# Squared-ReLU MLP of a two-block network: products of all 512 tokens, a freer boundary, and smaller settings

## The chip, the cores and the metric

The kernel runs on one core of a Trainium2 chip. Its five engines are TensorE (PE in the profile; its loads of the stationary operand are the row PEld), VectorE (DVE), ScalarE (ACT), GpSimd (POOL) and SyncE (SP), which issues most of the weight transfers. The metric is the device time of one execution in microseconds (us); lower is better. Everything is in 32-bit floats. TensorE multiplies in a shorter format, so each operand is kept as two parts, a rounded one (`hi`) and the rest (`lo`), and each product is three matmuls: hi x hi, hi x lo and lo x hi.

## The reference

Two transformer blocks run one after the other on 512 tokens of width 1024. The first has two attention forms side by side, attention to a memory and a SwiGLU MLP; the second has an mLSTM mixer, a squared-ReLU MLP, latent attention (MLA) and a second squared-ReLU MLP. The second block's norms are shifted and scaled by rows that are worked out from a condition vector. What matters here:

```
def sqrelu_mlp(h, w1, w2):
    return jnp.square(jax.nn.relu(h @ w1)) @ w2          # 1024 -> 4096 -> 1024
...
        ada = cond @ ada_w[l] + ada_b[l]
        sh1, sc1, g1, sh2, sc2, g2 = jnp.split(ada, 6, axis=-1)
...
        x = x + g1[:, None, :] * rmsnorm(y, norm_g[l, 1])
        h = modulate(rmsnorm(x, norm_g[l, 2]), sh2, sc2)
        y = sqrelu_mlp(h, mlp_w1[l], mlp_w2[l])
        x = x + g2[:, None, :] * rmsnorm(y, norm_g[l, 3])
```

The MLP appears twice (l = 0 and l = 1), with its own weights each time. The change touches the up projection `h @ w1` of l = 0.

## The kernel before, in words

Tokens come in four tiles of 128 (t = 0 to 3), features in tiles of 128 (k). The residual stays in SBUF as `x[t]`. The normalised, transposed input of a stage, `h` or `hn`, is either an `HT` (all 512 tokens in each buffer) or an `HS` (tokens 0 to 255 and 256 to 511 in buffers of their own). Such buffers, and the split weight tiles, come from one pool of 14 large buffers (`s8`); `HT` takes four of them when tile 0 is put, `HS` two then and two with tile 2.

**Weights.** `pump` loads raw weight tiles in the order of use and plans their splitting into hi (ScalarE) and lo (VectorE): `split` for plain tiles (L307 and L308, or L317 and L318 with a gain), `split7` for the seven-product form (L341, L342, and sums of weight quarters in L345 and L361). `wcap` bounds the split tiles that are alive; `lc` sets it for the last down projection of an MLP. While `quiet` is set, one piece is emitted about every two products.

**Products.** `prod` (L447 to L449) issues three matmuls for each k. An up projection of a squared-ReLU MLP takes pairs of hidden tiles. The first pairs go through `relu_pairs`, in halves of 256 tokens at the boundary. The later ones, when `h` is an `HS`, go through `wino`: the product of a 2 x 2 grid of blocks in seven products instead of eight, each of 4 k x 3 matmuls of 256 columns (L510), whose results VectorE and ScalarE combine (L520 to L534); `quarters` prepares the sums of token quarters, partly on GpSimd (L482). The choice stands in two lines:

```
        toks = (slice(0, 256), slice(256, S)) if halves or isinstance(h, HS) else (ALL,)
...
                by7 = k0 and isinstance(h, HS)
```

The 32 hidden tiles come in blocks of 6, 8, 6, 6 and 6; behind each block's up projection stands its part of the down projection, with sums in `acc` (L1358). The first block is always computed by `relu_pairs`.

**Boundaries.** `boundary` runs the last products of a stage tile by tile: `a` updates the residual (L648) and computes the next norm (squares L579, then GpSimd L568 and L562), `scaled` scales the row (L598), `put` transposes it on TensorE (L608), applies gain and shift if there are any (L616 on VectorE, L619 on ScalarE) and splits it (L626, L627). Products of the next stage (`first`) come between. Before, all of it stands inside `ordered()`: the order of PE, ACT, DVE and POOL is the written one. Outside such a region the framework's scheduler orders each engine's instructions by priority and a simulated time; `hot("hb")` raises the priority by 300 instructions.

**Row steps.** `ada` works out the condition rows in the background: `row_by` multiplies and adds weight rows on VectorE (L863), sums over partitions by one matmul (L881) and writes the row to DRAM; `cols_steps` reads some rows back as columns (transpose L386, copy L388). `step` makes one background step each time the products since the last have cost more than `pace` (`pacb` from the mLSTM on), except while `quiet` is set. `crow` and `gcol` force the steps that are still missing.

`all` calls the stages in order; the part that the change touches begins at `self.late = True`.

Of the kernel before, what the change touches and what calls it, by code (L numbers as in the profile page):

```python
# [20 lines left out]
P = 128  # L21
S = 512
NT = 4
DM = 1024
KD = 8
# [5 lines left out]
D_FF = 2816  # L31
ALL = slice(0, S)

BUF = dict(s8=14, u2=15, row=2, raw=4, w0=4, w1=4, w2=4, w3=5, w4=5, w5=5, w6=5, w7=5, ps=8, pace=2.0, pacb=2.0, man=0, lag=3, lagx=3, lagm=3, half=1, quiet=1, xp=0, fp=2, r1=1.25, r1b=3.6, r1c=2.4, r2=1.6, r2b=2.6, rx=1.4, rm=0.6, pre=10, gl=3, pl=0, hb=300, hs=0, ha=0, sp=0, spq=1.3, sq=1, b1=1, b2=1, lc=7, ar=4, mb=(6, 8, 6, 6, 6), mc=(4, 3, 4, 4, 4), st2=1, pr2=8, z1=4.5, z2=5, gt=3, rv=2, gs=1, rl=3, n1=4, ex=2, em=3, vg=1, sb=(8, 8, 6), mo=4, x1=2, g0=20, st=1, y1=0, y2=1, y3=0, ph=0, pq=0, fy=1, u1=6, s32=4, sm=60)

TWO_PI = 2.0 * np.pi

# [1 line left out]
def tt(t):  # L39
    return slice(t * P, (t + 1) * P)  # L40
# [98 lines left out]
class Net:  # L139
# [52 lines left out]
    def hot(self, key):  # L192
        n = BUF[key]
        return nullcontext() if self.dry or not n else self.tc.high_priority(offset=n)
# [181 lines left out]
    def cols_steps(self, name, srcs, eng=None):  # L376
        n = sum(k for _, k in srcs)
        r = self.u2((n, P))
        o = 0
        for src, k in srcs:  # L380
            (eng or self.nc.gpsimd).dma_start(out=r[o:o + k, :], in_=src.rearrange("(k p) -> k p", p=P))
            o += k
        for _ in range(3):
            yield None
        ps = self.bank((P, n))
        self.nc.tensor.transpose(out=ps, in_=r, identity=self.ident[:n, :n])  # L386
        c = self.t(f"cols_{name}", [P, n], F32, 1)
        self.nc.vector.tensor_copy(out=c, in_=ps)  # L388
        yield c
# [211 lines left out]

    def put(self, ys, h, k, t, mod=None):

        for y, cw in ys:
            n = cw // P
            ps = self.bank((P, n, P))
            for j in range(n):
                self.nc.tensor.transpose(out=ps[:, j, :], in_=y[:, tt(j)], identity=self.ident)  # L608
            hi, lo = h.blk(k, n, tt(t))
            if mod:  # L610
                g, sh = mod
                y = self.u2((P, n, P))
                for j in range(n):
                    gj, sj = (c[:, k + j:k + j + 1] for c in (g, sh))
                    if j < 2:
                        self.nc.vector.tensor_scalar(out=y[:, j, :], in0=ps[:, j, :], scalar1=gj, scalar2=sj,  # L616
                                                     op0=ALU.mult, op1=ALU.add)
                    else:
                        self.nc.scalar.activation(y[:, j, :], ps[:, j, :], AF.Identity, scale=gj, bias=sj)  # L619
                ps = y  # L620
            self.parts(hi, lo, ps)
            k += n

    def parts(self, hi, lo, x, scale=None):
        if scale is None:
# [5 lines left out]
                                                op0=ALU.mult, op1=ALU.subtract)  # L631


    def boundary(self, y_of, nxt, first, late=(1, 1, 2)):

# [3 lines left out]
        pend, rs = {}, {}  # L641
# [11 lines left out]
        def scaled(t):  # L653
            pend[t] = nxt(t, rs[t])

        with self.ordered():
            for t in range(NT):
                g, n = y_of(t), 0
                while True:
                    try:  # L660
                        next(g)
                    except StopIteration as e:
                        ys, ss = e.value
                        break
                    n += 1
                    if n == 4 and nxt and t >= 2:
                        self.put(*pend.pop(t - 2))
                if nxt and t >= 1:
                    scaled(t - 1)
                rs[t] = a(t, ys, ss)  # L670
            if nxt:
                i = -1
                for i, need in enumerate(first):
                    if i == late[0]:
                        scaled(NT - 1)
                    for n, t in ((1, NT - 2), (2, NT - 1)):
                        if i == late[n]:
                            self.put(*pend.pop(t))
                assert not pend, (i, late)
        self.quiet = False  # L680

# [379 lines left out]
    def mixer1(self):  # L1061
        nc, V, a = self.nc, self.nc.vector, self.a
        w = a["w_in"][0]
        self.x = [self.const(f"x{t}", [P, DM]) for t in range(NT)]
        get = lambda t: nc.sync.dma_start(out=self.x[t], in_=a["x"][0, tt(t), :])
# [8 lines left out]
            nc.sync.dma_start(out=ext[:, 64:256], in_=rb)  # L1074
            nc.sync.dma_start(out=far, in_=rb[:, 191:192].rearrange("h o -> (h o)").partition_broadcast(P))

        self.before = {2: [lambda: get(1)], 4: [lambda: get(2), lambda: get(3)], 6: [biases]}
        h = HT(self, KD)
        vf = self.big([P, NT, S])
        with self.in_order():  # L1080
# [7 lines left out]
        c = self.u2((8, S))  # L1088
# [104 lines left out]
        for t in range(NT):  # L1193
            ys = []
# [136 lines left out]
        return ho  # L1331


    def mlp(self, blocks, up, w_down, g, nxt, first, ready=None, caps=None):

        nc, V = self.nc, self.nc.vector
        acc = [[self.u2() for _ in range(2)] for _ in range(NT)]
# [1 line left out]
        for b, nb in enumerate(blocks):  # L1339
# [26 lines left out]
            if last:  # L1366
# [6 lines left out]
                        ms += part(t, c, (yield from product(t, wgs[c])))  # L1373
                    return acc[t], ms

                self.boundary(y_of, nxt, first)
            else:
                for c in range(2):
                    wg = self.weights(w_down, k0, nb, c * S, S)
# [59 lines left out]
    def relu2(self, h, l, g, nxt, first, ready=None):  # L1439
# [23 lines left out]
                quarters.extend(self.quarters(h))  # L1463

        quarters = []
        self.mlp(BUF['mb'], up, self.a["mlp_w2_2"][l], g, nxt, first, ready, BUF['mc'])


    VW = 129
# [408 lines left out]
    def all(self):  # L1878
# [13 lines left out]
        h = hn  # L1892
# [13 lines left out]
        self.late = True  # L1906
        self.cap(5)
        g = self.crow(2)
        hn = HS(self, KD)
        self.out_lin(a["a_w_out_2"][0], ho, g, nxt(4, 3, hn), self.relu_pairs(hn, a["mlp_w1_2"][0], 0, BUF["fp"], True), "head")  # L1910
        self.dumps(4)
        h = hn
# [64 lines left out]
```

## Time and profile before

| | |
|---|---|
| median of 3 runs | 2026.44 us (2026.16 to 2029.08) |
| the profiled execution's own time | 2028.55 us |
| its span, first to last instruction | 2026.5 us |
| mean granted clock of TensorE | 0.985 |
| busy: TensorE, VectorE, ScalarE, GpSimd | 1943.2, 1373.4, 1073.1, 355.6 us |
| moved by DMA | 242.01 MB, 119 GB/s |

The profiled execution lies 2.1 us above the median of the runs, and its time 2.05 us above its span. Matmuls overlap in the profile, so a busy TensorE is not one at its peak: what it could save shows as idle time before an instruction, and as a granted clock under 1. Stretches of the span in this kernel: SwiGLU MLP about 480 to 836, mLSTM 836 to 1030, its output and boundary 1030 to 1112, first squared-ReLU MLP 1112 to 1441, its boundary to 1482, MLA to 1633, its output and boundary to 1688, second squared-ReLU MLP to the end.

### The profile page before, as it was taken

The page shows a single profiled execution, that of the slowest core. Times are in us where ns is not written, and L with a number is a line of the kernel's source. Part 1 is how long each engine was busy: PE and PEld are TensorE (multiplying, and loading weights), DVE is VectorE, ACT ScalarE, POOL GpSimd, SP SyncE. Part 2 cuts the span into 40 slices and gives each one's busy share as a digit, 9 for nine tenths or more (in the row PEclk, how much of TensorE's full clock was granted, in tenths as well). Part 3 has the DMA queues.
Part 4 walks back from the last instruction along what each step waited for, and adds up shares of the span by engine and source line. Part 5 has one row for each costly group of instructions (what it writes and reads, how often), then busy time and mean ns, then how long its engine had stood idle before and what let it go on. Part 6 is the DMA issues. An engine that isn't in the chain of part 4 may idle for free. (4 is left out here: it accounts for less than half of the span.)

```text
span 2026.5 us, 29742 instructions
## 1 busy us (share of the span) xinstructions
PE 1943.2 (96%) x10738; PEld 1663.4 (82%) x10738; DVE 1373.4 (68%) x2689; ACT 1073.1 (53%) x2355; POOL 355.6 (18%) x711
## 2 busy tenths in 40 slices
PE   7999999999999999899999899998889989999997
PEld 5888988878888888678888788888687879989996
DVE  5756655856666665576866888898568747657665
ACT  6767775545353243556446464455465556545543
POOL 1331111201122211121323221222120012000000
PEclk9999999999999999999999999999999999999999
DMA  6322342523465554153442354565243212233321
GB/s 198 89 79 65 113 136 74 187 73 115 136 208 177 161 172 116 52 169 101 154 135 84 110 162 138 185 188 165 62 114 94 84 63 73 73 114 105 104 85 62
DMA packets 175251, 242.01 MB, mean 119 GB/s; under 512 B 20108, under 2 KB 117537, under 8 KB 175105
## 3 DMA queue, kind: packets, MB, share of 16 engines
q1 hardware_dynamic: 150704, 170.53, 27.2%
q0 software_dynamic: 24400, 69.60, 11.5%
q8 instruction: 84, 1.38, 0.3%
q14 instruction: 63, 0.51, 0.1%
HBM read 237.88 MB, written 2.20 MB: 118 GB/s over the span
## 5 line engine op out<-in xcount | busy, mean ns | idle before, releaser
L447 PE MATMUL ps<-s,s 128*128 128x512 f32 (+4 forms) x2276 | 863.0, 381 | 26.7 <-ACT s L626 25.1
L448 PE MATMUL ps<-s,s 128*128 128x512 f32 (+4 forms) x2276 | 851.6, 375 | 2.8 <-DVE s L627 1.9
L449 PE MATMUL ps<-s,s 128*128 128x512 f32 (+4 forms) x2276 | 849.7, 375 | 1.5 <-DVE s L627 1.4
L447 PEld LDWEIGHTS ps<-s,s 128*128 128x128 f32 (+2 forms) x2276 | 432.0, 190 | 105.9 <-ACT s L626 31.0
L449 PEld LDWEIGHTS ps<-s,s 128*128 128x128 f32 (+2 forms) x2276 | 431.2, 190 | 83.2 <-DVE s L627 5.2
L448 PEld LDWEIGHTS ps<-s,s 128*128 128x128 f32 (+2 forms) x2276 | 432.3, 190 | 79.1 <-DVE s L627 4.0
L510 PEld LDWEIGHTS ps<-s,s 128*128 128x128 f32 x2184 | 261.8, 188 | 6.7 <-DVE u L526 4.5
L510 PE MATMUL ps<-s,s 128*128 128x256 f32 x2184 | 263.7, 281 | 3.6 <-DVE u L526 3.6
L307 ACT ACTIVATE s<-raw 128x512 fp32r<-128x512 f32 x277 | 157.8, 622 | 143.2 <-PE ps L449 97.9
L308 DVE TENSOR_TENSOR s<-raw,s 128x512 fp32r<-128x512 f32 x277 | 190.3, 726 | 57.0 <-ACT s L307 55.7
L863 DVE SCALAR_TENSOR_TENSOR u<-araw,cond,u 128x512 f32<-128x512 f32 x224 | 167.3, 747 | 24.2 <-DMA araw<-in_ada_w 15.4
L317 ACT ACTIVATE s<-raw,cols_all 128x256 fp32r<-128x256 f32 (+1 forms) x305 | 143.5, 546 | 66.5 <-PE ps L449 29.8
L318 DVE SCALAR_TENSOR_TENSOR s<-raw,cols_all,s 128x256 fp32r<-128x256 f32 (+1 forms) x305 | 147.6, 538 | 39.3 <-ACT s L317 38.7
L868 POOL DMA_DIRECT2D araw<-in_ada_w x192 | 104.0, 542 | 338.0 <-DVE u L863 289.2
L627 DVE TENSOR_TENSOR s<-u,s 128x512 fp32r<-128x512 f32 x126 | 87.0, 700 | 79.4 <-ACT s L626 56.7
L626 ACT ACTIVATE s<-u 128x512 fp32r<-128x512 f32 x126 | 77.6, 625 | 63.8 <-PE ps L449 31.9
L568 POOL TENSOR_SCALAR sm<-sm,sm 128x1 f32<-128x1 f32 x34 | 10.5, 307 | 527.5 <-ACT junk L579 527.4
L341 ACT ACTIVATE s<-raw 128x512 fp32r<-128x512 f32 x104 | 62.7, 621 | 72.7 <-PE ps L449 37.6
L627 DVE TENSOR_TENSOR s<-ps,s 128x512 fp32r<-128x512 f32 (+3 forms) x100 | 59.1, 606 | 42.4 <-ACT s L626 35.0
L341 ACT ACTIVATE s<-u 128x512 fp32r<-128x512 f32 x78 | 48.7, 624 | 66.8 <-DVE u L345 36.4
L342 DVE TENSOR_TENSOR s<-raw,s 128x512 fp32r<-128x512 f32 x104 | 70.7, 683 | 15.4 <-ACT s L341 15.1
L1358 DVE TENSOR_TENSOR u<-ps,u 128x512 f32<-128x512 f32 x80 | 53.9, 685 | 34.3 <-PE ps L449 33.6
(261 smaller groups left out, 2162.9 us busy)
## 6 DMA issues: line engine op xcount, KB each, us to landing
raw<-in_mlp_w SPq DMA_DIRECT2D x128, 512.0 KB, 3.8
araw<-in_ada_w POOLq DMA_DIRECT2D x192, 256.0 KB, 3.5
raw<-in_w_gate_up SPq DMA_DIRECT2D x44, 512.0 KB, 4.1
raw<-in_w_in SPq DMA_DIRECT2D x24, 512.0 KB, 4.2
raw<-in_a_w_in SPq DMA_DIRECT2D x24, 512.0 KB, 3.8
raw<-in_w_down SPq DMA_DIRECT2D x22, 512.0 KB, 3.7
raw<-in_w_mem_kv SPq DMA_DIRECT2D x16, 512.0 KB, 3.6
araw<-in_kv_ada_w POOLq DMA_DIRECT2D x32, 256.0 KB, 4.0
```

The costliest lines, as they stand in the source:

```text
L307: A.activation(hi[:, sl, cl], src[:, sl, cl], AF.Copy)
L308: f.tensor_tensor(out=lo[:, sl, cl], in0=src[:, sl, cl], in1=hi[:, sl, cl].bitcast(F32), op=ALU.subtract)
L317: A.activation(hi[:, i, :], src[:, i, :], AF.Copy, scale=g)
L318: V.scalar_tensor_tensor(out=lo[:, i, :], in0=src[:, i, :], scalar=g, in1=hi[:, i, :].bitcast(F32), op0=ALU.mult, op1=ALU.subtract)
L341: A.activation(hi, x, AF.Copy)
L447: self.nc.tensor.matmul(ps, lhsT=ah, rhs=bh, start=first and i == 0, stop=False)
L448: self.nc.tensor.matmul(ps, lhsT=ah, rhs=bl, start=False, stop=False)
L449: self.nc.tensor.matmul(ps, lhsT=al, rhs=bh, start=False, stop=last and i == n - 1)
L510: nc.tensor.matmul(ps, lhsT=l[:, k, :], rhs=m[:, k, :], start=first and k == e == 0, stop=k == 3 and e == 2, skip_group_check=True)
L627: self.nc.vector.tensor_tensor(out=lo, in0=x, in1=hi.bitcast(F32), op=ALU.subtract)
L863: V.scalar_tensor_tensor(out=acc, in0=raws.pop(j), scalar=vec[:, j:j + 1], in1=acc, op0=ALU.mult, op1=ALU.add)
L868: nc.gpsimd.dma_start(out=raws[j], in_=ws[:, j, :])
```

## The change

In `BUF`, `pace` and `pacb` go from 2.0 to 1.9 and `lc` from 7 to 6. `cols_steps` lets five steps pass instead of three between reading a row and transposing it. `put` scales both halves of a tile, in the buffers they came in, before it splits the first. `boundary` gets a form without a written order (`fixed=False`), which the first squared-ReLU MLP's boundary uses; there the scaling of the last tile comes before the next stage's first product, and a tile is put when a product needs it. The x tiles are loaded one weight load earlier at the start. `hn` of the first squared-ReLU MLP becomes an `HT`, so its `relu_pairs` after the boundary take all 512 tokens in one product, and `wino` and `quarters` are no longer used there. The second MLP keeps them.

```diff
...
-        for _ in range(3):
+        for _ in range(5):
             yield None
...
     def put(self, ys, h, k, t, mod=None):
 
+        todo = []
         for y, cw in ys:
             n = cw // P
             ps = self.bank((P, n, P))
             for j in range(n):
                 self.nc.tensor.transpose(out=ps[:, j, :], in_=y[:, tt(j)], identity=self.ident)
-            hi, lo = h.blk(k, n, tt(t))
             if mod:
                 g, sh = mod
-                y = self.u2((P, n, P))
+                y = y.rearrange("p (n c) -> p n c", c=P)
...
                 ps = y
+            todo.append((k, n, ps))
+            k += n
+        for k, n, ps in todo:
+            hi, lo = h.blk(k, n, tt(t))
             self.parts(hi, lo, ps)
-            k += n
...
-    def boundary(self, y_of, nxt, first, late=(1, 1, 2)):
+    def boundary(self, y_of, nxt, first, late=(1, 1, 2), fixed=True):
...
-        with self.ordered():
+        hot = nullcontext if fixed else lambda: self.hot("hb")
+        with self.ordered() if fixed else nullcontext():
             for t in range(NT):
                 g, n = y_of(t), 0
...
-                    if n == 4 and nxt and t >= 2:
+                    if n == 4 and nxt and t >= 2 and fixed:
                         self.put(*pend.pop(t - 2))
-                if nxt and t >= 1:
-                    scaled(t - 1)
-                rs[t] = a(t, ys, ss)
+                with hot():
+                    if nxt and t >= 2 and not fixed:
+                        self.put(*pend.pop(t - 2))
+                    if nxt and t >= 1:
+                        scaled(t - 1)
+                    rs[t] = a(t, ys, ss)
             if nxt:
-                i = -1
+                if not fixed:
+                    with hot():
+                        scaled(NT - 1)
                 for i, need in enumerate(first):
-                    if i == late[0]:
+                    if fixed and i == late[0]:
                         scaled(NT - 1)
-                    for n, t in ((1, NT - 2), (2, NT - 1)):
-                        if i == late[n]:
-                            self.put(*pend.pop(t))
+                    for t in sorted(pend):
+                        if t <= need if not fixed else i >= late[t - 1]:
+                            with hot():
+                                self.put(*pend.pop(t))
...
-        self.before = {2: [lambda: get(1)], 4: [lambda: get(2), lambda: get(3)], 6: [biases]}
+        self.before = {1: [lambda: get(1)], 3: [lambda: get(2), lambda: get(3)], 6: [biases]}
...
-    def mlp(self, blocks, up, w_down, g, nxt, first, ready=None, caps=None):
+    def mlp(self, blocks, up, w_down, g, nxt, first, ready=None, caps=None, fixed=True):
...
-                self.boundary(y_of, nxt, first)
+                self.boundary(y_of, nxt, first, fixed=fixed)
...
-        self.mlp(BUF['mb'], up, self.a["mlp_w2_2"][l], g, nxt, first, ready, BUF['mc'])
+        self.mlp(BUF['mb'], up, self.a["mlp_w2_2"][l], g, nxt, first, ready, BUF['mc'], fixed=nxt is None)
...
         g = self.crow(2)
-        hn = HS(self, KD)
+        hn = HT(self, KD)
         self.out_lin(a["a_w_out_2"][0], ho, g, nxt(4, 3, hn), self.relu_pairs(hn, a["mlp_w1_2"][0], 0, BUF["fp"], True), "head")
```

## Rows read from the trace of the kernel before

**Rows 1.** The page: busy us of each engine, share of the span, instructions.

```profile
PE 1943.2 (96%) x10738; PEld 1663.4 (82%) x10738; DVE 1373.4 (68%) x2689; ACT 1073.1 (53%) x2355; POOL 355.6 (18%) x711
```

**Rows 2.** Windows: length, busy us (instructions) PE, PEld, DVE, ACT, POOL, clock, DMA.

```profile
630.00:680.00 50.00, 50.00 (x218) 40.52 (x217) 30.39 (x52) 15.89 (x32) 8.95 (x18) 1.00 0.47 149
1089.00:1115.00 26.00, 25.94 (x222) 25.73 (x220) 16.95 (x22) 17.55 (x34) 12.27 (x8) 1.00 0.29 90
1121.00:1441.00 320.00, 304.27 (x1813) 267.94 (x1814) 269.61 (x458) 153.63 (x288) 68.29 (x130) 0.97 0.51 157
1688.00:1987.00 299.00, 295.80 (x1886) 267.23 (x1886) 202.81 (x343) 157.60 (x293) 9.87 (x6) 1.00 0.30 92
```

**Rows 3.** Waits of TensorE from 1112 to 1441: us in total, times, longest.

```profile
PE ps L386 <- DMA u<-arow: 5.8, 2, 4.7
PE ps L447 <- ACT s L626: 5.5, 3, 3.3
PE ps L881 <- DVE u L627: 4.4, 2, 3.6
PE ps L510 <- DVE u L526: 3.6, 3, 1.7
PE ps L449 <- DVE s L627: 1.4, 1, 1.4
```

**Rows 4.** Waits of TensorE from 1441 to 1482.

```profile
PE ps L608 <- ACT u L598: 8.8, 2, 7.5
```

**Rows 5.** Windows around the longest waits, columns as in rows 2.

```profile
1117.00:1125.00 8.00, 4.06 (x11) 3.25 (x12) 7.83 (x13) 1.45 (x3) 1.51 (x3) 0.57 0.01 1
1407.00:1412.00 5.00, 4.78 (x15) 3.83 (x16) 4.15 (x9) 1.09 (x3) 1.01 (x3) 0.66 0.59 177
1417.00:1429.00 12.00, 7.20 (x19) 4.80 (x18) 8.85 (x15) 4.85 (x11) 2.14 (x4) 0.57 0.68 204
1469.00:1480.00 11.00, 5.67 (x25) 5.68 (x26) 5.96 (x21) 5.23 (x12) 1.33 (x4) 0.53 0.62 144
```

**Rows 6.** Chain of waits in the second MLP: start, us, what.

```profile
1887.64 25.44 PE ps L510 x216
```

**Rows 7.** Groups of VectorE from 1121 to 1441: busy us, mean ns, idle before.

```profile
L342 DVE TENSOR_TENSOR s<-raw,s 128x512 fp32r<-128x512 f32 x52 | 35.4, 681 | 4.7 <-ACT s L341 4.6
L308 DVE TENSOR_TENSOR s<-raw,s 128x512 fp32r<-128x512 f32 x52 | 33.7, 684 | 0.4
...
L345 DVE TENSOR_TENSOR u<-u,raw 128x512 f32<-128x512 f32 x13 | 8.9, 682 | 0.1
...
L532 DVE SCALAR_TENSOR_TENSOR u<-ps,u 128x256 f32<-128x256 f32 x13 | 5.4, 417 | 4.5 <-PE ps L510 4.5
```

**Rows 8.** Timeline at the boundary behind the MLP: start, us, instruction, idle before.

```profile
1465.50 0.56 POOL L562 TENSOR_TENSOR sm<-sm,mhalf 128x1 f32<-128x1 f32 x1
...
1471.07 0.49 DVE L1693 TENSOR_TENSOR u<-ps,row 128x320 f32<-128x320 f32 x1 [3.21 <-DMA row<-arow]
...
1473.57 1.32 ACT L598 ACTIVATE u<-x,sm 128x512 f32<-128x512 f32 x2
```

**Rows 9.** Timeline of puts and first products at the boundary before the MLP.

```profile
1073.23 0.81 ACT L619 ACTIVATE u<-ps,cols,cols 128x128 f32<-128x128 f32 x2 [1.54 <-DVE u L616]
...
1076.16 0.81 ACT L619 ACTIVATE u<-ps,cols,cols 128x128 f32<-128x128 f32 x2 [1.46 <-DVE u L616]
...
1089.36 0.36 PE L447 MATMUL ps<-s,s 128*128 128x256 f32 x1
...
1094.01 0.63 ACT L626 ACTIVATE s<-u 128x512 fp32r<-128x512 f32 x1
```

**Rows 10.** Timeline at the boundary after the memory attention, ScalarE.

```profile
459.30 0.60 ACT L626 ACTIVATE s<-ps 128x512 fp32r<-128x512 f32 x1 [2.85 <-PE ps L449]
```

**Rows 11.** Waits of TensorE at the SwiGLU boundary, 805 to 870.

```profile
PE ps L447 <- ACT s L307: 1.2, 1, 1.2
```

**Rows 12.** Waits of TensorE from 0 to 40.

```profile
PE ps L447 <- ACT s L626: 4.8, 2, 3.9
```

More of the change, by code (lines that the diff above doesn't have):

```diff
@@ L32 @@
 ALL = slice(0, S)
-BUF = dict(s8=14, u2=15, row=2, raw=4, w0=4, w1=4, w2=4, w3=5, w4=5, w5=5, w6=5, w7=5, ps=8, pace=2.0, pacb=2.0, man=0, lag=3, lagx=3, lagm=3, half=1, quiet=1, xp=0, fp=2, r1=1.25, r1b=3.6, r1c=2.4, r2=1.6, r2b=2.6, rx=1.4, rm=0.6, pre=10, gl=3, pl=0, hb=300, hs=0, ha=0, sp=0, spq=1.3, sq=1, b1=1, b2=1, lc=7, ar=4, mb=(6, 8, 6, 6, 6), mc=(4, 3, 4, 4, 4), st2=1, pr2=8, z1=4.5, z2=5, gt=3, rv=2, gs=1, rl=3, n1=4, ex=2, em=3, vg=1, sb=(8, 8, 6), mo=4, x1=2, g0=20, st=1, y1=0, y2=1, y3=0, ph=0, pq=0, fy=1, u1=6, s32=4, sm=60)
+BUF = dict(s8=14, u2=15, row=2, raw=4, w0=4, w1=4, w2=4, w3=5, w4=5, w5=5, w6=5, w7=5, ps=8, pace=1.9, pacb=1.9, man=0, lag=3, lagx=3, lagm=3, half=1, quiet=1, xp=0, fp=2, r1=1.25, r1b=3.6, r1c=2.4, r2=1.6, r2b=2.6, rx=1.4, rm=0.6, pre=10, gl=3, pl=0, hb=300, hs=0, ha=0, sp=0, spq=1.3, sq=1, b1=1, b2=1, lc=6, ar=4, mb=(6, 8, 6, 6, 6), mc=(4, 3, 4, 4, 4), st2=1, pr2=8, z1=4.5, z2=5, gt=3, rv=2, gs=1, rl=3, n1=4, ex=2, em=3, vg=1, sb=(8, 8, 6), mo=4, x1=2, g0=20, st=1, y1=0, y2=1, y3=0, ph=0, pq=0, fy=1, u1=6, s32=4, sm=60)
 TWO_PI = 2.0 * np.pi
```

## The prediction

> **What bounds the kernel now.** I read the page first: TensorE is busy for 96% of the span and no other engine for more than 68% [rows 1]. So a change pays only through work taken off TensorE or through time in which TensorE stands still or runs at half clock. Second, busy time by stretch [rows 2]: in the SwiGLU MLP TensorE has no idle time at all while VectorE is busy for 61%; in the second squared-ReLU MLP, which runs the seven-product form without a background of ada rows, it is busy for 295.80 of 299.00 us beside VectorE at 68%; in the first one, from 1121 to 1441, it is busy for 304.27 of 320.00 us, with VectorE at 84%. The reader should see that the same TensorE code has idle time only where VectorE is that full. Third, the waits of TensorE in that MLP, counted from 1112 to take in its first matmuls [rows 3]: 20.7 us in the five largest groups, for the cols transpose (L386), the hidden block (L626, L627), the row sums (L881) and the combination of the seven products (L526). Fourth, the waits at the boundary behind it: 8.8 us, all for the scaled residual (L598) [rows 4]. Fifth, the granted clock around these waits [rows 5]: it lies between 0.53 and 0.66 in four short stretches, so part of each ran at 1.2 GHz, each time after TensorE had stood still or had been halting. TensorE's busy time there times what the clock lacked is 4.06 x 0.43 + 4.78 x 0.34 + 7.20 x 0.43 = 6.5 us in the MLP and 5.67 x 0.47 = 2.7 us at the boundary. What can be had back is thus at most 27.2 us in the MLP and 11.5 us at the boundary.
>
> **The up projection (the dear part).** After the first block 26 hidden tiles, 13 pairs, change form. A pair was 7 products x 4 x 3 = 84 matmuls of 256 columns; it becomes 2 x 8 x 3 = 48 matmuls of 512. In an unbroken run 216 of the first took 25.44 us, 0.1178 each [rows 6]; the full stretch 630 to 680 holds 218 matmuls of 512 columns, one of them cut by the edge, so 50.00 / 217 = 0.2304 each [rows 2]. A pair goes from 9.90 to 11.06 us, and 13 pairs cost 13 x 1.16 = 15.1 us more. Twice the columns cost 1.96 times as much, so nothing is won by the longer form itself.
>
> **What it takes off VectorE.** Per pair 7 subtractions of the weight parts (L342), 4 sums of weight quarters (L345 and L361) of 0.68 us and 5 combinations of 0.42 us (L532 and four like it) go; 4 plain weight subtractions of 0.68 us (as L308) come [rows 7]. That is 7 x 0.68 + 4 x 0.68 + 5 x 0.42 - 4 x 0.68 = 6.9 us a pair, 89 us in all. VectorE falls from 269.6 us to about 181 in some 330, or 55%: below the 61% and 68% at which the two other MLPs run with 0 and 3.2 us of idle TensorE. The preparation of the token quarters goes too, and with it four large buffers. The 3.6 us for L526 go for certain, as the instruction is gone. The waits for L626, L627 and L881 (11.3 us) are for VectorE or ScalarE work that stands in a queue, which gets shorter. The wait for L386 is for a small transfer, and the transpose is issued two steps later than now. I keep 5 of the 27.2 us as lost (the other squared-ReLU MLP also keeps 3.2) and take -22. The bounds are -27.2, all of it, and -3.6, L526 alone.
>
> **The boundary behind this MLP.** The norm of the last token tile is there at 1465.50 + 0.56. In the written order its scaling stands on ScalarE behind the square of the first latent row, which waits for VectorE, which waits for a bias row that lands at 1471; the scaling starts at 1473.57 only [rows 8]. That is the 7.5 us wait. With `fixed=False` the scaling comes before the next stage's first product, the put of tile 3 behind the product of tile 2, and the scheduler, not a written order, queues the rest. I take -9 of the 11.5 us. The bounds are -11.5 and, if the free order puts weight pieces ahead of the chain, a loss of +4, half of that wait again.
>
> **The boundary before this MLP.** `hn` becomes HT, and the third up pair is now a product of all 512 tokens, so it can no longer start on tokens 0 to 255. In the trace TensorE is busy for 25.94 of 26.00 us there [rows 2]. After the last transposes 24 matmuls (2.8 us from 1089.4) are ready without tile 3; its first split ends at 1094.01 + 0.63 [rows 9]. So a hole of 2.4 us opens: +2.5. If the second half of tile 3, a chain of 2.93 us later, is waited for too, it is about 6; if the new put is quicker, 0. HT also wants four of the 14 large buffers at once, beside 4 of `ho` and 8 of weights: 16. The split of tile 0's second half must then wait until weights are released, and behind it on ScalarE stand the square and scaling of the next tile, for which the transposes wait. The boundary after the memory attention has these same sizes. Its split waited there for 2.85 us [rows 10], of which I charge TensorE 0.5, with bounds of 0 and 2.85.
>
> **put.** With gain and shift, the second half's scaling starts 1076.16 - 1073.23 = 2.93 us after the first's, behind its split [rows 9]. The new order scales both halves first: the first split is 0.81 us later, the second about 1.5 us earlier. Three boundaries use it, and TensorE waits for both halves. I take -2 in all, with bounds of -4 and +2.
>
> **lc, the start, the row step.** With lc=6 one split weight tile less stands ready at two boundaries. Its two pieces are 1.4 us on VectorE by L308 [rows 7], and at the first of them TensorE already waits 1.2 us for such a piece [rows 11]: +1, bounds 0 and +3. The x tiles come one weight load earlier, which helps puts that cost 4.8 us at the start [rows 12] and delays the weights of the last two k: 0, bounds -4 and +3. Two more yields in ten cols steps are 20 more row steps; 1.9 for 2.0 over some 340 is 17 sooner. The rows end where they did; no deadline is moved: 0. If it were, a burst of steps would stand before a boundary; I bound that by the 5.8 us that TensorE waits for L386.
>
> **Sum.** 15.1 - 22 - 9 + 2.5 + 0.5 - 2 + 1 = -13.9 us. Against the profiled execution's 2028.55 us this gives 2014.7; against the median of the runs shown, 2026.44, it gives 2012.5. I predict 2014 us.
>
> **Rivals.**
> 1. The waits belong to the ada rows, not to the seven products. For: L386 and L881 are row work (10.2 us), and the rows keep their steps. Against: the SwiGLU stage carries the same rows with no idle time. Then only 3.6 us come back: 15.1 - 3.6 - 9 + 2.5 + 0.5 - 2 + 1 = +4.5, or 2033, slower. It decides for slower than before as soon as less than 8.1 us are recovered in the MLP.
> 2. The boundary's wait only moves: in the free order the bias row or weight pieces hold the chain up as long, and its 9 us stay. For: all of ScalarE, VectorE and GpSimd is shared there. Against: what held the scaling up is now issued after it. The sum is -4.9, or 2023.7, at the edge of no change.
> 3. All of it comes back: 15.1 - 27.2 - 11.5 + 0 - 4 = -27.6, or 2001.
> 4. A 512-column product in a dense run costs no more than one of 256. Then a pair takes 48 x 0.1178 = 5.65 us, the first term is -55, and the time about 1944. The 0.2304 us of a run without a gap speaks against it.
>
> The Trainium skill, "TensorE: Matmul & The Clock Gate", section "Back-to-back issue gap", gives 131 ns for a matmul of 512 columns in a sustained stream. By that the 13 pairs would take 82 us. The full stretch above, at 0.2304 us each, does not agree with that figure; its other formula there, columns over 2.4 GHz plus 2.5 ns, makes the first term 15.4 us.
>
> **Chances.** Forecast (2005 to 2021) 0.51; rival 2 (2021 to 2028) 0.18; rival 1 (2028 to 2042) 0.16; rival 3 (under 2005) 0.14; rival 4 0.01. A measurement here tells some 0.2%, 4 us, from no change. Faster than 2022.4 takes the forecast, rivals 3 and 4 and a third of rival 2: 0.72. Within 4 us are most of the rest of rival 2 and the near edge of rival 1: 0.14. Slower has 0.14. The range, 2002 to 2030, leaves out about a tenth on each side: the far end of rival 3, and rival 1 beyond its near edge with the bounds of the unknown costs on top.
>
> **What would show it.** After: no L510 before the second MLP; TensorE idle under 6 us between the first MLP's first product of all tokens and its last product, VectorE at 50 to 60%; products of 0.230 to 0.235 us; the granted clock full there; the wait for L598 at the boundary under 3 us; a new hole of 2 to 3 us before the MLP's first full product. The prediction is wrong if TensorE still waits for L386, L881 or L626 by more than 10 us in this MLP, if the free boundary costs more than the written one, or if the start or the SwiGLU boundary loses more than 3 us.

## The result and the profile after

The changed kernel takes 2000.64 us (median of 4 runs, 2000.26 to 2001.97) beside 2027.67 for the kernel before in the same series (4 runs, 2026.16 to 2029.08): a ratio of 0.9868, 95% interval 0.9851 to 0.9885. It is 27 us faster. The forecast was 2014, 14 us faster, with a range from 2002 to 2030, so the time lies below the range. The direction was right, and so was most of the mechanism in the MLP and at its boundary; half of the gain was missing from the sum.

First the page of the changed kernel, the line that answers to [rows 1]: busy us, share of the span (1998.9 us), instructions.

```profile
PE 1948.0 (97%) x10222; PEld 1647.1 (82%) x10222; DVE 1285.3 (64%) x2517; ACT 1036.1 (52%) x2282; POOL 347.5 (17%) x703
```

TensorE is busy 5 us longer in a span 28 us shorter: the change took idle time and half-clock time, not work. VectorE lost 88 us; the prediction counted 89 for the MLP.

Busy time by stretch, columns as in [rows 2]: the end of the boundary before the first squared-ReLU MLP, that MLP, its boundary, a piece of the MLP with matmuls of 512 columns (two row sums among them), the SwiGLU with its boundary, the mLSTM with its output, the MLA, and a piece of the mLSTM.

```profile
1096.00:1117.00 21.00, 20.81 (x151) 18.95 (x149) 10.96 (x21) 14.21 (x27) 0.00 (x0) 1.00 0.33 102
1117.00:1438.00 321.00, 321.00 (x1385) 259.66 (x1386) 179.75 (x274) 124.42 (x221) 58.50 (x112) 1.00 0.44 140
1438.00:1475.00 37.00, 34.22 (x200) 31.57 (x199) 25.52 (x58) 25.77 (x55) 9.47 (x18) 0.95 0.45 116
...
1200.00:1250.00 50.00, 50.00 (x217) 40.42 (x216) 36.60 (x56) 13.23 (x24) 14.90 (x28) 1.00 0.67 216
...
475.00:859.00 384.00, 380.29 (x1709) 310.96 (x1708) 267.10 (x468) 152.98 (x323) 89.40 (x173) 0.99 0.51 161
859.00:1096.00 237.00, 225.67 (x1123) 186.35 (x1122) 169.34 (x319) 129.09 (x281) 60.05 (x102) 0.97 0.43 131
...
1475.00:1628.00 153.00, 152.06 (x871) 133.29 (x869) 97.51 (x266) 90.03 (x222) 7.39 (x17) 1.00 0.23 73
...
888.00:900.00 12.00, 8.09 (x23) 6.40 (x24) 8.82 (x12) 2.73 (x4) 5.28 (x10) 0.72 0.27 83
```

The MLP has no idle TensorE and a full clock; VectorE is busy for 179.75 of 321 us, 56% (forecast: 55%). A matmul of 512 columns still takes 50.00 / 217 = 0.2304 us. The hole that was to open before the first product of all 512 tokens is not there: 20.81 of 21.00 us are busy.

The waits of TensorE after: the boundary behind the MLP, which answers to [rows 4], and the mLSTM (859 to 1060), which had shown nothing of note before.

```profile
PE ps L449 <- DVE s L630: 2.0, 1, 2.0
PE ps L447 <- ACT s L629: 0.8, 1, 0.8
...
PE ps L891 <- DVE u L630: 4.4, 1, 4.4
PE ps L609 <- DVE u L1623: 2.2, 1, 2.2
```

The 8.8 us for L598 are gone and 2.8 us for parts stand there. The last norm of that boundary ends on GpSimd at 1461.27, and its scaling starts at 1461.31, where before it waited from 1466.06 to 1473.57 [rows 8].

Between the same points of the program the stages last, in us. The points are the last tile's transposes at the boundaries before the SwiGLU, the mLSTM and the first MLP, the first product of the MLA's latent rows, the MLA's own first transposes, and the first and the last tile's transposes at its output boundary:

| stage | before | after |
|---|---|---|
| start to the memory attention's boundary | 475.8 | 474.8 |
| SwiGLU | 383.9 | 383.8 |
| mLSTM and its output | 228.9 | 236.9 |
| first squared-ReLU MLP | 368.5 | 354.6 |
| its boundary | 32.1 | 24.7 |
| MLA | 162.3 | 153.8 |
| its output boundary | 27.2 | 24.8 |
| second MLP | 347.9 | 345.5 |

Two lines were not in the sum at all: the mLSTM lost 8 us, the MLA won 8.5. Both are the row step, as the experiments will show. A step of the background (the work up to its next `yield`) is made by this code; the comment is mine:

```
        self.pace -= cost          # 0.65 a product, 0.34 in the seven-product form
        if self.pace < 0 and not self.quiet:
            self.pace = BUF["pacb" if self.late else "pace"]
            self.step_bg()
```

A product is here the three matmuls of one k, whatever their columns. A step comes after a whole number of products: four at 2.0 (2.6 is over 2.0, 1.95 is not), three at 1.9. So a step is a third denser, not 5%; in the seven-product form it is six products at either number. The busy time of the ada multiplications alone, which work out the condition rows (L863 before, L873 after), shows it by stretch: length, busy us (count), clock, DMA share, GB/s; first before, then after.

```profile
476.00:860.00 384.00, 59.89 (x80) 1.00 0.47 146
860.00:1088.00 228.00, 27.62 (x39) 0.99 0.43 133
1088.00:1457.00 369.00, 63.95 (x87) 0.97 0.46 143
1489.00:1651.00 162.00, 11.93 (x16) 0.99 0.31 93
```

```profile
475.00:859.00 384.00, 75.65 (x103) 0.99 0.51 161
859.00:1096.00 237.00, 29.27 (x39) 0.97 0.43 131
1096.00:1450.00 354.00, 53.83 (x72) 1.00 0.43 135
1475.00:1628.00 153.00, 0.00 (x0) 1.00 0.23 73
```

80 become 103 in the SwiGLU, and none is left for the MLA. The row sums (L881, now L891), one for each piece of a row, say when the rows end; count, min/median/max ns, first and last start; before, then after.

```profile
L881 PE MATMUL ps<-u,onesr x30: 307/394/503, 390.0 to 1633.1; 128*128 128x512 f32 x28, 128*128 128x320 f32 x1, 128*128 128x384 f32 x1
```

```profile
L891 PE MATMUL ps<-u,onesr x30: 314/395/796, 380.9 to 1344.7; 128*128 128x512 f32 x28, 128*128 128x320 f32 x1, 128*128 128x384 f32 x1
```

The rows end 288 us earlier. In the kernel before, the last of them comes only 18 us ahead of the MLA's output boundary (1651.4). The theory at this point: the MLP gave back all its waits, and the row step, in whole products, moved the rows out of the MLA at a price in the mLSTM. The rivals: the step is only 5% quicker and the MLA gained by something else; the MLP gained from the thinner rows, not from the product form.

### The profile page after: what moved, and what is told of

Read it like the earlier page. It is cut to its first block, busy times and chain, and to the rows that moved or that the text cites. A ratio compares the mean times of both kernels' runs of the same rounds, so it can differ in the third digit from the quotient of the medians.

```text
span 1998.9 us, 28470 instructions
## 1 busy us (share of the span) xinstructions
PE 1948.0 (97%) x10222; PEld 1647.1 (82%) x10222; DVE 1285.3 (64%) x2517; ACT 1036.1 (52%) x2282; POOL 347.5 (17%) x703
## 4 chain that ended last, share of the span: by engine, by line
PE 88%; DVE 4%; ACT 4%; issue 2%; POOL 1%; DMA 1%; SPq 0%; DVEq 0%; POOLq 0%; ACTq 0%
PE ps L447 24%; PE ps L448 24%; PE ps L449 24%; PE ps L510 6%; PE ps L1033 1%; PE ps L609 1%; PE ps L1823 1%; PE ps L1852 1%; PE ps L1004 1%; PE ps L1583 1%; PE ps L1017 1%; DVE s L318 1%; DVE s L630 1%; ACT s L629 1%; ACT s L317 1%
## 5 line engine op out<-in xcount | busy, mean ns | idle before, releaser
L447 PE MATMUL ps<-s,s 128*128 128x512 f32 (+3 forms) x2468 | 942.8, 383 | 19.3 <-ACT s L629 19.1
L448 PE MATMUL ps<-s,s 128*128 128x512 f32 (+3 forms) x2468 | 930.0, 377 | 2.1 <-DVE s L630 1.8
L449 PE MATMUL ps<-s,s 128*128 128x512 f32 (+3 forms) x2468 | 927.6, 377 | 2.8 <-DVE s L630 2.8
L447 PEld LDWEIGHTS ps<-s,s 128*128 128x128 f32 (+1 forms) x2468 | 467.3, 190 | 106.5 <-ACT s L629 24.0
L449 PEld LDWEIGHTS ps<-s,s 128*128 128x128 f32 (+1 forms) x2468 | 466.9, 189 | 93.2 <-DVE s L630 4.7
L448 PEld LDWEIGHTS ps<-s,s 128*128 128x128 f32 (+1 forms) x2468 | 468.1, 190 | 86.8 <-DVE s L630 3.6
L307 ACT ACTIVATE s<-raw 128x512 fp32r<-128x512 f32 x329 | 186.3, 622 | 177.6 <-PE ps L449 130.0
L308 DVE TENSOR_TENSOR s<-raw,s 128x512 fp32r<-128x512 f32 x329 | 221.1, 712 | 88.6 <-ACT s L307 86.9
L873 DVE SCALAR_TENSOR_TENSOR u<-araw,cond,u 128x512 f32<-128x512 f32 x224 | 168.4, 752 | 27.7 <-DMA araw<-in_ada_w 18.8
L317 ACT ACTIVATE s<-raw,cols_all 128x256 fp32r<-128x256 f32 (+1 forms) x305 | 143.2, 545 | 59.3 <-issue 24.9
L510 PEld LDWEIGHTS ps<-s,s 128*128 128x128 f32 x1092 | 130.4, 189 | 1.0
L510 PE MATMUL ps<-s,s 128*128 128x256 f32 x1092 | 130.7, 280 | 0.0
L568 POOL TENSOR_SCALAR sm<-sm,sm 128x1 f32<-128x1 f32 x34 | 12.6, 369 | 668.0 <-ACT junk L579 540.2
L629 ACT ACTIVATE s<-u 128x512 fp32r<-128x512 f32 x118 | 71.7, 628 | 54.1 <-PE ps L449 28.7
L1465 ACT ACTIVATE u<-ps 128x512 f32<-128x512 f32 x38 | 22.6, 595 | 102.9 <-PE ps L449 99.0
L629 ACT ACTIVATE s<-ps 128x512 fp32r<-128x512 f32 (+3 forms) x100 | 51.0, 525 | 24.8 <-PE ps L609 7.0
L318 DVE SCALAR_TENSOR_TENSOR s<-raw,cols_mix,s 128x128 fp32r<-128x128 f32 (+2 forms) x152 | 52.5, 401 | 12.5 <-ACT s L317 12.1
```

Of the source, the lines that this page charges most:

```text
L307: A.activation(hi[:, sl, cl], src[:, sl, cl], AF.Copy)
L308: f.tensor_tensor(out=lo[:, sl, cl], in0=src[:, sl, cl], in1=hi[:, sl, cl].bitcast(F32), op=ALU.subtract)
L317: A.activation(hi[:, i, :], src[:, i, :], AF.Copy, scale=g)
L318: V.scalar_tensor_tensor(out=lo[:, i, :], in0=src[:, i, :], scalar=g, in1=hi[:, i, :].bitcast(F32), op0=ALU.mult, op1=ALU.subtract)
L447: self.nc.tensor.matmul(ps, lhsT=ah, rhs=bh, start=first and i == 0, stop=False)
L448: self.nc.tensor.matmul(ps, lhsT=ah, rhs=bl, start=False, stop=False)
```

## The experiments

All are timed against the kernel before, in the same series (its median 2027.2 to 2027.6).

**1. The step, three products or four.** The changed kernel with 1.96 for 1.9.

```diff
-pace=1.9, pacb=1.9
+pace=1.96, pacb=1.96
```

> The changed kernel with pace and pacb at 1.96 instead of 1.9. Theory: a row step comes after a whole number of products of cost 0.65, three at 1.9 and four at 1.96 as at 2.0. So the row sums in the SwiGLU MLP go from 21 us apart back to 28, row work stands in the latent attention again (some 8 us more there), the mLSTM stretch gets some 7 us back, and the time is 2001 to 2009. Rival: the step goes with the number itself, 3% between 1.9 and 1.96; then the sums are about 21.7 us apart, all rows still end before the latent attention, and the time is 2000 to 2002.

Measured: 2014.41 us, ratio 0.9935 (0.9920 to 0.9949). 3% in the number cost 14 us, so the step is counted in whole products; the linear rival falls. The row sums stand 28 us apart again and the mLSTM takes 226.4 us. But it went further than I expected: now the last row sum comes at 1683.4 and the MLA takes 174.9. TensorE's waits from 1600 to 1660:

```profile
PE ps L891 <- DVE u L630: 11.6, 1, 11.6
PE ps L386 <- DMA u<-arow: 5.6, 1, 5.6
PE ps L447 <- ACT s L629: 5.3, 1, 5.3
```

The rows are late at the MLA's output boundary, where the next gain and shift must be there, and the steps that are left are forced there. The rows are this late because the changed kernel also has 20 more steps (its yields, experiment 7) and fewer products that count (experiment 5).

**2. Four products up to the mLSTM, three behind it.** `pacb` holds from the mLSTM's output on: `self.late` is set behind the mLSTM itself.

```diff
-pace=1.9, pacb=1.9
+pace=2.0, pacb=1.9
```

> The changed kernel with the old row step (2.0) up to the end of the mLSTM and the new one (1.9) after it. Theory: the 8 us that the mLSTM stretch lost come from row steps that the new row step moved into it, and the 8.5 us that the latent attention won come from rows that are done before it; so the loss goes and the gain stays, 1992 to 1996. Rival: the mLSTM stretch lost its time to the smaller lc or to put, and nothing moves: 1999 to 2002.

Measured: 1997.44 us, 0.9849 (0.9834 to 0.9863). The mLSTM is back at 227.6 us, without its waits, so its loss belongs to the denser step there. I had expected the MLA's gain to stay; it did not: the rows reach into the MLA again (last sum 1538.3; 164.8 us), and the time is 1.4 us above the expected range. Loss and gain of the step sit in different stages; experiments 7 and 8 have the one without the other.

**3. The changed kernel with the seven-product form.**

```diff
-        hn = HT(self, KD)
+        hn = HS(self, KD)
         self.out_lin(a["a_w_out_2"][0], ho, g, nxt(4, 3, hn), ...)
```

> The changed kernel with the seven-product form kept in the first squared-ReLU MLP (HS instead of HT), all else as changed. Theory: the TensorE waits of that MLP belong to the seven-product form beside the rows; they come back (up to 27 us) and 15 us of products go: 2008 to 2016. Rival: the waits went because the row step changed, and the longer products only cost: 1984 to 1990.

Measured: 2009.61 us, 0.9910 (0.9895 to 0.9925); the first MLP takes 368.4 us, as before. Its waits:

```profile
PE ps L891 <- DVE u L630: 7.5, 1, 7.5
PE ps L386 <- DMA u<-arow: 5.9, 1, 5.9
PE ps L510 <- ACT u L530: 4.4, 1, 4.4
PE ps L510 <- DVE u L526: 3.2, 3, 1.1
```

Leaving the seven-product form is what frees this MLP, also of the waits for row work (L891, L386), and five yields don't cure L386: it waits 5.9 us beside 5.8 in [rows 3]. The rival with the thinner rows falls: 72 ada multiplications stand in this MLP, as many as in the changed kernel.

**4. The written order at the boundary behind the MLP.**

```diff
-..., ready, BUF['mc'], fixed=nxt is None)
+..., ready, BUF['mc'], fixed=True)
```

> The changed kernel with the written order at the boundary behind the first squared-ReLU MLP (fixed=True). Theory: the scaling of the last token tile stands behind the first latent row again, TensorE waits some 7 us for L598 and part of it runs at half clock: 2006 to 2010. Rival: the wait went because other work there got lighter or earlier, and the order does not matter: 1999 to 2003.

Measured: 2009.16 us, 0.9912 (0.9895 to 0.9928). Boundary and MLA together take 189.9 us beside 178.5. The waits from 1440 to 1480:

```profile
PE ps L447 <- ACT s L317: 5.0, 1, 5.0
PE ps L447 <- ACT s L629: 2.2, 1, 2.2
```

The written order costs 8.5 us here, but not by the wait for L598 that I expected: what is late is a weight piece (L317). The free order is worth its term even with the row step changed.

**5. The product form alone, on the kernel before.**

```diff
-        hn = HS(self, KD)
+        hn = HT(self, KD)
```

> The kernel before with the product form of the first squared-ReLU MLP alone (HT in place of HS); the written boundary, lc=7, three yields and a step of 2.0 stay. If the seven-product form costs what the changed kernel's own run without it showed, the first MLP falls from 368.5 to 353 to 357 us, its boundary keeps 28 to 32 us, the memory attention, SwiGLU and mLSTM stages keep their lengths within 2 us, and the time is 2011 to 2018. Rival: in the changed kernel the longer form is only cheap because the quicker row steps had already taken the ada rows away; then TensorE waits for L386 and L881 stay in this MLP by over 10 us and the time is 2024 to 2034.

Measured: 2029.2 us, ratio 1.0006 (0.9997 to 1.0016): no gain. This was the surprise. The time is in the rival's range, but not by its waits: none for L386 or L881 is left in this MLP. The MLP's part of the theory holds: 355.9 us, and no idle TensorE in the second window below. The gain was lost in the first one, behind the MLA's output boundary.

```profile
1666.00:1702.00 36.00, 26.89 (x166) 25.58 (x165) 21.54 (x37) 17.52 (x35) 3.78 (x8) 0.76 0.37 117
1117.00:1438.00 321.00, 321.00 (x1391) 259.77 (x1390) 181.67 (x281) 126.67 (x227) 59.60 (x114) 1.00 0.45 143
```

Before, the same 36 us behind the last tile's transposes were nearly full and at full clock:

```profile
1678.00:1714.00 36.00, 34.23 (x261) 32.72 (x260) 27.25 (x37) 22.91 (x43) 11.28 (x7) 1.00 0.29 89
```

The waits of experiment 5 there (1666 to 1702), and its ada multiplications by stretch (MLP, MLA, behind the boundary):

```profile
PE ps L447 <- ACT s L626: 4.0, 1, 4.0
PE ps L881 <- DVE u L627: 3.8, 1, 3.8
PE ps L448 <- DVE s L627: 1.2, 1, 1.2
...
1088.00:1445.00 357.00, 52.22 (x71) 1.00 0.43 136
1477.00:1639.00 162.00, 17.84 (x24) 0.99 0.38 111
1666.00:1702.00 36.00, 5.94 (x8) 0.76 0.37 117
```

The rows are late: last row sum at 1695.3, after the boundary (1633.1 before). A pair in seven products holds 28 counts of 0.34, six to a step: 4.67 steps. In full products it holds 16 counts of 0.65, four to a step: 4. Thirteen pairs make 8.7 steps fewer. The third pair of the first block, which an HS multiplies in two halves of 256 tokens, adds to that: each half counts 0.65 a product too, so 32 counts become 16, eight steps four. Together 12.7 steps are gone. A step of four products is twelve matmuls of 0.2304 us, 2.8 us, so by my estimate the rows end some 35 us later, and only 18 us were left. Where row 11 is asked for, right behind the boundary, `crow` forces the steps that are missing. By the window, 36.00 - 26.89 = 9.1 us of standing still (1.8 before) and 26.89 x 0.24 = 6.5 us of missing clock (none before) are lost; the second MLP's stage is 15.1 us longer, and the first MLP's 12.6 are gone.

**6. The step alone, on the kernel before.**

```diff
-pace=2.0, pacb=2.0
+pace=1.94, pacb=1.94
```

> The kernel before with the row step alone at 1.94 in place of 2.0 (three products a step in place of four, by the count of 0.65 a product). If the step is a whole number of products, row sums in the SwiGLU stand 21 us apart (28 before), the last one comes before 1400 (1633 before), the mLSTM stage grows from 228.9 to 235 to 239 us, the MLA stage falls from 162.3 to 153 to 156, the first MLP, where VectorE is busy for 84%, grows by 0 to 8, and the time is 2024 to 2036: no gain by itself. If a step of 1.94 is only 3% quicker, every stage keeps its length within 2 us and the row sums stay 28 us apart.

Measured: 2033.56 us, ratio 1.0030 (1.0020 to 1.0039): slower by itself. mLSTM 238.2 (+9.3), MLA 153.8 (-8.5), as expected, and the first MLP 373.3 (+4.8), where VectorE is busy for 261.23 of 320 us (82%) with the seven-product form and the rows. Its largest wait from 1117 to 1480:

```profile
PE ps L881 <- DVE u L627: 16.8, 3, 10.2
```

**7. Three yields, step 2.0 and 1.9.** Experiment 2 with the old number of yields.

```diff
-        for _ in range(5):
+        for _ in range(3):
```

> The changed kernel with a step of 2.0 up to the mLSTM's output and 1.9 behind it, as in the run before, and three yields in place of five in the cols step. If the extra yields are what carried the ada rows into the MLA there (20 row steps of 2.1 us), the last row sum comes some 40 us earlier, at 1490 to 1510, the MLA stage falls from 164.8 to 155 to 160 us, and the time is 1988 to 1995, with no wait for L386 above 3 us. If the two yields hide the cols transfer, its wait comes back in several places (L386 over 5 us in all) and the time is 1997 to 2004.

Measured: 1989.08 us, 0.9807 (0.9792 to 0.9822), 11.6 us under the changed kernel and 8.4 under experiment 2. The last row sum comes at 1471.9, 66 us earlier and sooner than I expected, and the MLA takes 154.1 us. The row sums, and the one wait of TensorE for a row's transfer:

```profile
L891 PE MATMUL ps<-u,onesr x30: 307/393/402, 389.4 to 1471.9; 128*128 128x512 f32 x28, 128*128 128x320 f32 x1, 128*128 128x384 f32 x1
...
PE ps L386 <- DMA u<-arow: 0.6, 1, 0.6
```

So two yields in each cols step are pure delay of the rows here, worth 8 us where they push the rows over a stage's edge, and with the products of 512 tokens the small transfer doesn't need them.

**8. Four products up to the mLSTM, two behind it.**

```diff
-pace=1.9, pacb=1.9
+pace=2.0, pacb=1.29
```

> The changed kernel with a step of 2.0 (four products) up to the mLSTM's output and 1.29 (two products) behind it. If the mLSTM's loss is four-for-three and the MLA's gain is that no row work is left there, the mLSTM stage is 226 to 229 us, the last row sum comes before 1400, the MLA stage is 153 to 156, and the time is 1987 to 1993. Rival: row work twice as dense fills VectorE in the first MLP (56% busy in the changed kernel) above the 84% at which it made TensorE wait; then the first MLP grows from 354.6 to 360 or more and the time is 1995 to 2005.

Measured: 1992.1 us, 0.9825 (0.9810 to 0.9839). mLSTM 227.8, last row sum 1343.4, MLA 153.8, as the theory says; the first MLP grows to 358.6, with a wait of 2.4 us for L386 and, at the boundary behind it, a clock of 0.87 (1439 to 1466). The rival was half right: the denser steps cost 4 us, not 5 and more. With 111 ada multiplications there (87 before), the products of 512 tokens still leave the MLP 10 us shorter than before.

**9. The product form and the step together, on the kernel before.**

```diff
-pace=2.0, pacb=2.0
+pace=1.94, pacb=1.94
...
-        hn = HS(self, KD)
+        hn = HT(self, KD)
```

> The kernel before with two edits only: the product form of the first MLP and a step of 1.94 (three products) throughout; the written boundary, lc=7 and three yields stay. Alone the form moved the time by +0.06% and the step by +0.3%. If the form alone failed because its pair holds 16 products, four steps of the background, in place of 28 short ones, 4.67 steps, so that the ada rows ran on into the last boundary and cost there what the MLP gave, then the quicker step pays just that: first MLP 353 to 358 us, mLSTM 235 to 239, MLA 153 to 156, second MLP 345 to 349, and the time is 2008 to 2018. If the two edits only add, the time is 2030 to 2038.

Measured: 2019.05 us, 0.9958 (0.9946 to 0.9971), 8.2 us faster, where +2.0 (within the noise) and +6.3 alone would add up to 8.3 slower. The rows end at 1310.1, the MLA takes 153.7 us and the second MLP 346.4, and the 36 us that lost the time in experiment 5 are full (first line below): the burst is gone, and the MLP keeps its gain (357.3). The edits only pay together: the form takes steps away, the quicker step gives them back. It is 1 us above the expected range: the boundaries are as slow as before, and here the hole before the first full product is there. The 36 us behind the last tile's transposes at the MLA's output boundary, TensorE's waits from 1080 to 1115, of which the hole is the second (2.8 us before 1105.28), and the window around it:

```profile
1668.00:1704.00 36.00, 35.85 (x269) 33.94 (x269) 27.41 (x38) 22.32 (x41) 10.53 (x7) 1.00 0.30 89
...
PE ps L447 <- ACT s L626: 6.1, 2, 3.3
...
1090.00:1117.00 27.00, 24.18 (x159) 22.55 (x158) 14.23 (x28) 15.73 (x32) 2.81 (x6) 0.90 0.32 98
```

**10. lc=7 in the changed kernel.** The edit is that number in the table of sizes.

> The changed kernel with lc=7, as before. The prediction put lc=6 at +1 (0 to 3), by a wait for a weight piece at the SwiGLU boundary. In the changed kernel's trace that boundary shows only the 2.8 us for the scaled residual, so I expect 1998 to 2002, no difference that can be told; if lc=6 cost the +1 to +3, the time is 1997 to 2000 and the SwiGLU stage is 1 to 3 us shorter.

Measured: 2002.97 us, 0.9882 (0.9868 to 0.9895). lc=7 is 2.3 us slower, but the intervals overlap, and the profiled difference (mLSTM 241.7 beside 236.9) isn't at the place that the prediction named. Not settled; a cost of lc=6 isn't seen.

**11. The old put in the changed kernel.** The loop that scales and splits a half before it turns to the next.

```diff
-        todo = []
...
+            hi, lo = h.blk(k, n, tt(t))
...
-                y = y.rearrange("p (n c) -> p n c", c=P)
+                y = self.u2((P, n, P))
...
-            todo.append((k, n, ps))
+            self.parts(hi, lo, ps)
             k += n
-        for k, n, ps in todo:
-            hi, lo = h.blk(k, n, tt(t))
-            self.parts(hi, lo, ps)
```

The scaled halves are then also in buffers of their own again; no run separates that from the order.

> The changed kernel with the old put, which scales and splits one half after the other. By the prediction's term of -2 in all (three boundaries) the time is 2001 to 2004, with the second half's split later by 1 to 2 us at the boundaries before the memory attention, the mLSTM and the two MLPs; if the order inside put is hidden behind other products, 1999 to 2002 and every stage within 1 us.

Measured: 2008.11 us, 0.9906 (0.9892 to 0.9919). The new put is worth 7.5 us, nearly four times the term, and the time is 4 us above the expected range. The first MLP's stage is 4.4 us longer with the old one and the MLA's output boundary 3.7. ScalarE at the boundary before the first MLP, tiles 2 and 3, with the old put:

```profile
1094.36 0.81 ACT L619 ACTIVATE u<-ps,cols,cols 128x128 f32<-128x128 f32 x2 [0.47 <-DVE u L616]
...
1100.22 0.81 ACT L619 ACTIVATE u<-ps,cols,cols 128x128 f32<-128x128 f32 x2 [1.46 <-DVE u L616]
1101.06 0.63 ACT L626 ACTIVATE s<-u 128x512 fp32r<-128x512 f32 x1
1103.14 0.81 ACT L619 ACTIVATE u<-ps,cols,cols 128x128 f32<-128x128 f32 x2 [1.46 <-DVE u L616]
1103.98 0.63 ACT L626 ACTIVATE s<-u 128x512 fp32r<-128x512 f32 x1
```

and with the new one:

```profile
1093.33 1.50 ACT L619 ACTIVATE u<-ps,cols,cols 128x128 f32<-128x128 f32 x4 [1.01 <-DVE u L616]
1094.72 1.16 ACT L629 ACTIVATE s<-u 128x512 fp32r<-128x512 f32 x2
1097.42 1.50 ACT L619 ACTIVATE u<-ps,cols,cols 128x128 f32<-128x128 f32 x4 [1.54 <-DVE u L616]
1098.80 1.16 ACT L629 ACTIVATE s<-u 128x512 fp32r<-128x512 f32 x2
```

The old order goes to and fro between VectorE and ScalarE once for each half, a period of 2.92 us, and tile 3 starts 5.86 us behind tile 2; the new one goes once for each tile, and tile 3 starts 4.09 us behind. Counted from tile 2's transposes (1091.21 and 1091.85), the last split ends after 13.40 us with the old put and after 8.11 with the new. TensorE needs tile 3's first half first: with the old put it waits 2.9 us for the split that ends at 1101.69, and its clock falls to half behind that (0.89 in the mean from 1095 to 1110, beside 1.00); with the new one it doesn't wait. The hole of the prediction is real, and put is what closes it.

**12. The old start in the changed kernel.**

```diff
-        self.before = {1: [lambda: get(1)], 3: [...], 6: [biases]}
+        self.before = {2: [lambda: get(1)], 4: [...], 6: [biases]}
```

> The changed kernel with the x tiles loaded behind the second and fourth weight loads again, as before. The prediction put this edit at 0 (-4 to +3); the changed kernel's start stage was 1.0 us shorter than before. If that is this edit, the start stage is 475 to 477 us and the time 2000 to 2003; the waits for L629 in the first 40 us are the place to see it (5.4 us in two in the changed kernel, 4.8 in two before).

Measured: 2000.77 us, 0.9870 (0.9854 to 0.9885): nothing. The start takes 475.6 us, 0.8 longer than in the changed kernel, but the time doesn't follow, and the profiled starts of the runs here lie between 472.4 and 475.8 with either order.

## Where the prediction was right, and where it failed

The time is below the range because two terms were too small: the waits of the MLP, and put with the hole that it closes. The row step, which stood in the sum as 0, has the wrong mechanism, but its number came out nearly right. The terms beside what undoing or isolating them measured (medians, us):

| part | predicted | measured |
|---|---|---|
| product form, its waits, the hole, the large buffers (0.5), and the row step | 15.1 - 22 + 2.5 + 0.5 + 0 = -3.9 | -8.2 (experiment 9) |
| boundary behind the MLP | -9 | -8.5 (experiment 4) |
| put | -2 | -7.5 (experiment 11) |
| lc | +1 | -2.3, within the intervals (experiment 10) |
| start | 0 | -0.1 (experiment 12) |
| sum | -13.9 | -26.6 of -27.0 |

That the right column adds up so well is in part luck: its first row is measured on the kernel before and the others on the changed one, and the -2.3 of lc is not clear of noise.

**The product form: right, its waits mis-sized.** 0.2304 us a matmul, VectorE at 56%, no L510 before the second MLP, a full clock. The -22 kept 5 of the 27.2 us of [rows 3, 5] as lost, and that was too cautious: the window shows no idle time, and experiment 5's MLP is 12.6 us shorter with matmuls that cost 15.1 more, so about -27.7 came back, the hole included. That also settles rival 1, which is wrong, though experiments 3 and 6 show a grain of it: in this MLP the row work waits beside the seven-product form, and otherwise only in experiment 8 (2.6 us), where it is densest. A matmul of 512 columns at 131 ns, as the Trainium skill has it in "TensorE: Matmul & The Clock Gate", section "Back-to-back issue gap", was not seen here either: 0.2304 us in 50 us without a gap.

**The boundary behind it: right** (-8.5 for -9).

**The row step: the mechanism that failed.** "Two more yields in ten cols steps are 20 more row steps; 1.9 for 2.0 over some 340 is 17 sooner. The rows end where they did; no deadline is moved: 0." The 20 are right, the rest is not. The step is a whole number of products, four or three, so it is a third denser, not 5%; the product form removes 12.7 steps that I didn't count, as I costed the pairs on TensorE and VectorE only, not what they count for in the background; and the deadline behind the MLA is close enough that either decides. The burst that I bounded by 5.8 us costs 15.1 (experiment 5). The net of it in the changed kernel is small, +8.0 in the mLSTM and -8.5 in the MLA, which hid it: that the 0 came out nearly right is luck. Without the quicker step the form alone is worth nothing (experiment 5).

**put: the mis-sized term.** I took -2 for put and +2.5 for the hole, as two terms, though I wrote that a quicker put would close the hole. The half-tile period of 2.93 us that I read in [rows 9] (2.92 in experiment 11) repeats for every half of tiles 2 and 3 in a row, TensorE waits at the end of that chain, and the clock falls behind the wait. It is one chain: put is worth -7.5, not -2, and the hole of +2.5 doesn't open. With -27.7 for -22, -7.5 for -2 and no hole, the prediction's own sum is -27.6; measured are -27.0.

**The sum and rival 3.** The time, 2000.64, is that of rival 3 (2001), and so are two of its reasons: the MLP's waits all came back, and no hole opened. The other two missed it on either side and nearly cancel, which is luck: the boundary gave 8.5 of its 11.5 us, put 7.5 in place of 4.

What stays open: what five yields do at a step of 1.9 (the remainder, 0.4 us, is no measurement); why lc=7 lengthens the mLSTM in its one profile; why a denser step makes the first row sum in the mLSTM wait 4.4 us, other than that it stands 33 us behind the boundary and is gone with four products a step.

A version faster than both: experiment 7, 1989.08 us, 38 us under the kernel before.

## What to carry to other kernels

Background work that is paced by a count of foreground work is part of each edit's cost: count how many steps the edited code carries, round as the code rounds, and find the deadline that comes after the last step; an edit can give its gain at one place and pay it back hundreds of us later. A chain that goes to and fro between two engines costs its period for each piece, so order the pieces engine by engine, and cost the whole row of pieces up to the instruction that waits for the last. Parts of a change that gain nothing or lose alone can win together: here +2.0, which is no more than noise, and +6.3 make -8.2.

## What was not expected of the hardware

The loss behind a late row is mostly not the wait of its row sum. In experiment 5 the row sum waits 3.8 us; the window of 36 us around it loses 9.1 us of standing still and 6.5 us at a granted clock of 0.76. In the changed kernel the 4.4 us wait in the mLSTM has a clock of 0.72 around it (888 to 900), where before TensorE was busy for all 12 us at 1.00:

```profile
888.00:900.00 12.00, 12.00 (x53) 9.75 (x52) 8.52 (x13) 6.89 (x11) 1.58 (x3) 1.00 0.14 37
```
